# State-space outputs woven into the second attention, with one operand laid out in DRAM beforehand

## The chip, the cores and the metric

The kernel runs on one core of a Trainium2 chip. The metric is the device time of one execution in microseconds (us); the time of a kernel is the median of several executions. TensorE (PE) multiplies matrices into PSUM, ScalarE (ACT) applies functions and copies, VectorE (DVE) does elementwise work and reductions, GpSimd (POOL) does some elementwise work and issues DMAs, and SyncE (SP) issues most DMAs. Each engine runs its own instructions strictly in order and waits on semaphores of the others.

## The reference, cut to what matters

Two blocks follow one another on 512 rows of 1024 columns. The first has two layers (windowed attention, gated linear attention), each with an MLP. The second block mixes an attention and a state-space model through gates, then runs a mixture of experts. The part that the change touches is the middle of the second block:

```python
h = rms_norm_2(x, mix_norm_gain[i])
proj = h @ w_in[i]
...
gate = jax.nn.sigmoid(proj[..., 3 * D_ATTN + D_SSM:] + b_gate[i])
gate = gate.reshape(bsz, l, N_BRANCH, D_MODEL)
y_attn = chunked_relpos_attention(q, k, v, q_gain[i], k_gain[i], rel_bias[i])
y_ssm = s5_ssm_glu(u, ssm_lambda_re[i], ssm_lambda_im[i], ...)
wb = w_branch[i]
merged = (gate[:, :, 0] * (y_attn @ wb[:D_ATTN])
          + gate[:, :, 1] * (y_ssm @ wb[D_ATTN:]))
x = x + merged @ w_out[i]
```

`chunked_relpos_attention` has 8 heads: scores plus a bias, softmax, values. `s5_ssm_glu` runs a linear recurrence over time, reads its outputs out of the states and the inputs, and applies `z = gelu(y)`, then `z * sigmoid(z @ w_glu + b_glu)`.

## The kernel before

All products run as three matmuls of a split pair (`hi` and `lo`), so every 1 MB weight unit is loaded by SP (L214), cast by ACT (`whi`, L221) and subtracted by DVE (`wlo`, L222) before TensorE uses it (L240 to L252). Two `raw`, two `whi` and two `wlo` buffers are in turn. A scheduler with a timeline of its own fixes, when the kernel is built, the order of instructions on each engine; the program's order and Python generators give it the candidates, and on the chip each engine then follows its list in order.

**Constants.** `SSM.constants` is a generator that the second MLP steps through as filler. It leaves in DRAM the tables `w1`, `g` and `k`; `k` has the shape [16, 32, 15, 16] and holds the response of the state-space model to inputs within 8 time steps, with zeros for the future (L1344, and eight stores at L1347).

**Attention of the second block.** `block2_mix` first makes q, k, v and the recurrence's inputs, then runs eight heads. `scores(h)` loads the bias tile `tb` (SP, L1538), splits q and k (ACT L1542, L1545; DVE L1543, L1547), and in four steps multiplies (PE L1555, L1556), adds the bias and takes the maximum (DVE L1558), and takes the exponential (ACT L1563). `values` takes two heads: it scales the probabilities (DVE L1573), transposes them (PE L1581), copies them out of PSUM (ACT and DVE, L1582) and multiplies with V (PE L1585). Between these steps `gate_unit` computes the 16 gate tiles, 24 matmuls each on `hl`, and POOL stores them to DRAM (L1532). The loop asks for one gate tile in every second step of a head, so two for each head:

```python
for n, _ in enumerate(scores(h)):
    if n % 2:
        next(last, None)
    else:
        next(gen, None)
```

**Branches.** After the attention, `fetch` loads gate tiles back (SP, L1629; four buffers), and `branch` multiplies the attention's output `ya` with a branch weight, 12 matmuls for each of 8 rows of `mT`; ACT applies the sigmoid (L1637) and DVE the product (L1660). `ssm.load` brings `G` (two DMAs of 1 MB, L1405) and `W3` (eight DMAs of 256 KB, L1408, whose runs in DRAM are 512 bytes long) into SBUF. After rows 6 and 7 of `mT`, `ssm.outputs` computes the state-space outputs in two halves (Q = 0 and 1): TensorE multiplies the states with `G` (L1423) and the inputs with `W3` (L1427) into two banks, ACT and DVE copy them to `Y` (L1431), TensorE turns `Y` (L1435), and ACT applies gelu into `zT` (L1437). `parts` splits `zT` into the pair `z` (L1648, L1649). Then follow the products `z @ w_glu` with their sigmoid (48 matmuls), which give `ys`, the products of `ys` with the other branch weights (96 matmuls), the output projection and the mixture of experts.

Of the kernel before, what the change touches and what calls it, by code (L numbers as in the profile page):

```python
# [19 lines left out]
P = 128  # L20
# [1165 lines left out]
class SSM:  # L1186


    def __init__(self, K):
        self.K = K  # L1190
        self.w1 = K.dram.tile([P, 2, 16, P], F32, name="ssm_w1")
        self.g = K.dram.tile([P, 2, 16, P], F32, name="ssm_g")
        self.k = K.dram.tile([16, 32, 15, 16], F32, name="ssm_k")
        self.a8 = K.c.tile([P, 2, 2, 16], F32, name="ssm_a8")

    def constants(self, tp):
# [149 lines left out]
        for q in range(8):  # L1346
            nc.gpsimd.dma_start(self.k.rearrange("c (a q) l x -> q c a (l x)", q=8)[q][:, :, 7 * 16:],  # L1347
                                kk[16 * q:16 * q + 16])

    def inputs(self, zp, sp, u_rows):  # L1350

# [46 lines left out]

    def load(self, sp, between):

        nc = self.K.nc
        self.G = sp.tile([P, 2, 16, P], F32, name="ssm_g2", bufs=1)
        self.W3 = sp.tile([P, 32, P], F32, name="ssm_w3", bufs=1)
        for part in range(2):
            nc.sync.dma_start(self.G[:, part], self.g[:, part])  # L1405
        between()
        for t in range(8):
            nc.sync.dma_start(self.W3[16 * t:16 * t + 16].rearrange("p g (t c) -> p g t c", t=8),  # L1408
                              self.k[:, :, 7 - t:15 - t, :])

    def outputs(self, sp, Q, zT):

        K, Z, UT, G, W3 = self.K, self.Z, self.UT, self.G, self.W3
        nc, a, mm = K.nc, K.nc.scalar, K.nc.tensor.matmul
        b = [K.bank() for _ in range(2)]
        for ii in range(4):
            os = [(8 * Q + 4 * h + ii, [b[g][64 * h:64 * h + 64, ii * P:ii * P + P] for g in range(2)])
                  for h in range(2)]
            for part in range(2):
                for g in range(2):  # L1420
                    s = slice(64 * g, 64 * g + 64)
                    for i, o in os:
                        mm(o[g], Z[s, 0:64, part, i], G[s, part, i],  # L1423
                           start=part == 0, stop=False, skip_group_check=True)
            for g in range(2):
                for i, o in os:
                    mm(o[g], UT[:, 2 * i + g, :], W3[:, 2 * i + g, :],  # L1427
                       start=False, stop=True, skip_group_check=True)
        Y = sp.tile([P, 8, P], F32, tag="ssm_y", name=K.nm("Y"), bufs=1)
        for g, e in enumerate((a.copy, K.nc.vector.tensor_copy)):  # L1430
            e(Y.rearrange("p t (i g c) -> p g t i c", g=2, c=16)[:, g],  # L1431
              b[g].rearrange("p (i t c) -> p t i c", i=4, t=8))
        b = K.bank2()
        for t in range(8):
            nc.tensor.transpose(b[:, t * P:t * P + P], Y[:, t, :], K.ident)  # L1435
        for h in range(2):
            a.activation(zT[:, 2 * Q + h].rearrange("p (j t) -> p t j", t=8),  # L1437
                         b.rearrange("p (t h j) -> p h t j", t=8, h=2)[:, h], AF.Gelu_apprx_tanh)


def block2_mix(K, X, hl, ssm, out):
# [6 lines left out]
    with ExitStack() as left:  # L1448
# [85 lines left out]

        with K.right("at2", 2) as ap:
            def scores(h):
# [57 lines left out]

            def gates(c0, c1):
                for c in range(c0, c1):
                    yield from gate_unit(c)

            last, done, gen = iter(()), [], gates(0, 8)
            for h in range(8):  # L1600
                for n, _ in enumerate(scores(h)):
                    if n % 2:
                        next(last, None)
                    else:
                        next(gen, None)
                if h % 2:
                    for _ in last:
                        pass
                    last = values(*done[-2:])
# [5 lines left out]
        z_close.close()  # L1615

        K.h_close.close()
        K.sides = {"left": "left", "right": "right"}
# [23 lines left out]
        zs.push(sz_close)  # L1642
        gl = zs.enter_context(K.left("ssmz", 2))
        z = K.pair(gl, "z", [P, 4, L])

        def parts(Q):
            d = slice(2 * Q, 2 * Q + 2)
            return (nc.scalar.copy(z[0][:, d], zT[:, d]).ins,  # L1648
                    v.tensor_sub(z[1][:, d], zT[:, d], z[0][:, d].bitcast(F32)).ins)  # L1649

        with K.left("ssmr", 2) as sp:
            for r in range(4):
                fetch(r)
            ssm.load(sp, lambda: [fetch(r) for r in range(4, 8)])
            for c in range(2):
                w = K.unit(A["w_br"][c])
                for m in range(4):
                    f = 4 * c + m
                    b, g = branch(w, ya, m, f, f)
                    v.tensor_mul(mT[:, f, :], b, g)  # L1660
                    if c and m in (2, 3):
                        ssm.outputs(sp, m - 2, zT)
                        turned = parts(m - 2)
        yo = left.enter_context(K.left("b2o"))
# [449 lines left out]
```

## Time and profile before

| | us |
|---|---|
| runs of the kernel before | 2270.74, 2275.36, 2281.77 |
| median | 2275.36 |
| the profiled execution | 2268.23 |
| its span on the core | 2266.2 |

| engine | busy us | share of the span |
|---|---|---|
| PE (matmul) | 2138.9 | 94% |
| PEld (weight load) | 1769.3 | 78% |
| DVE | 1390.6 | 61% |
| ACT | 971.2 | 43% |
| POOL | 334.8 | 15% |

The profiled execution is 7.1 us under the median. The span runs from the first instruction to the last, and 2.0 us of the execution lie outside it. The busy share is an average over stages with different limits; what a stage is worth is read from the stretch of time that it covers, which the rows further below do. Times in rows are counted from the start of the span. The attention's gates end near 1861 us, its last value product near 1898 us, and the products on `ys` begin near 1957 us.

### The profile page before, as it was taken

To read this page: it belongs to the slowest core of one execution; us is meant where nothing else is said; L and a number is where in the kernel's file an instruction comes from. 1 tells how busy PE (TensorE), PEld (TensorE's weight loads), DVE (VectorE), ACT (ScalarE), POOL (GpSimd) and SP (SyncE) were. 2 spreads that over 40 slices of the span, in tenths; PEclk is the share of its full clock that TensorE was granted. 3 is DMA by queue.
4 is the path that set the end of the run, shared out by engine and by line. 5 is a ranking of instruction groups with operands and counts; after the bars stand their busy time and mean duration, and the time that the engine had idled before them with its cause. 6 is when DMAs were issued, how large, how long until landed. Compare 5 with 4: busy or idle time off the path is not lost. (4 is left out here: it accounts for less than half of the span.)

```text
span 2266.2 us, 30706 instructions
## 1 busy us (share of the span) xinstructions
PE 2138.9 (94%) x12088; PEld 1769.3 (78%) x12088; DVE 1390.6 (61%) x2436; ACT 971.2 (43%) x1512; POOL 334.8 (15%) x453
## 2 busy tenths in 40 slices
PE   7999999999999999999989999999899997897996
PEld 5876668888888888789977887888799874686875
DVE  4666654999644444631794597555646754547985
ACT  5446656421121222542554632322353453535874
POOL 0035622112000000510000000000220100012332
PEclk9999999999999999999999999999999998998998
DMA  7112231557321121211211224232322435468993
GB/s 291 64 39 98 82 149 38 195 189 255 122 75 56 56 75 56 72 38 59 93 38 38 88 93 149 106 104 84 120 94 94 154 122 115 174 237 278 331 298 105
DMA packets 57970, 279.12 MB, mean 123 GB/s; under 512 B 9248, under 2 KB 13744, under 8 KB 32992
## 3 DMA queue, kind: packets, MB, share of 16 engines
q1 hardware_dynamic: 38048, 219.39, 27.4%
q0 software_dynamic: 18768, 55.04, 7.7%
q10 hardware_dynamic: 1008, 2.70, 0.4%
q8 instruction: 96, 1.57, 0.3%
q14 instruction: 50, 0.41, 0.1%
HBM read 264.54 MB, written 24.08 MB: 127 GB/s over the span
## 5 line engine op out<-in xcount | busy, mean ns | idle before, releaser
L221 ACT CAST whi<-raw 128x2048 fp32r<-128x2048 f32 x106 | 202.4, 1909 | 559.3 <-PE b L252 389.1
L222 DVE TENSOR_TENSOR wlo<-raw,whi 128x2048 fp32r<-128x2048 f32 x106 | 246.0, 2322 | 223.4 <-ACT whi L221 222.1
L250 PE MATMUL b<-hl,whi 128*128 128x512 f32 (+1 forms) x736 | 284.1, 386 | 2.3 <-DVE t L323 1.5
L248 PE MATMUL b<-hl,whi 128*128 128x512 f32 (+1 forms) x736 | 283.0, 385 | 0.8 <-ACT whi L221 0.8
L252 PE MATMUL b<-hl,wlo 128*128 128x512 f32 (+1 forms) x736 | 281.6, 386 | 0.0
L815 DVE TENSOR_TENSOR acc<-acc,b 128x512 f32<-128x512 f32 x280 | 180.8, 682 | 156.0 <-PE b L252 155.7
L248 PE MATMUL b<-whi,hid 128*128 128x512 f32 x640 | 215.5, 395 | 2.5 <-ACT whi L221 1.9
L250 PE MATMUL b<-wlo,hid 128*128 128x512 f32 x640 | 216.8, 394 | 0.0
L252 PE MATMUL b<-whi,hid 128*128 128x512 f32 x640 | 215.1, 395 | 0.0
L250 PEld LDWEIGHTS b<-hl,whi 128*128 128x128 f32 x736 | 139.1, 189 | 30.3 <-issue 2.9
L248 PEld LDWEIGHTS b<-hl,whi 128*128 128x128 f32 x736 | 139.1, 189 | 30.1 <-ACT whi L221 1.3
L252 PEld LDWEIGHTS b<-hl,wlo 128*128 128x128 f32 x736 | 139.3, 189 | 28.3 <-issue 0.2
L1970 DVE TENSOR_TENSOR wlo<-raw,whi 128x2048 fp32r<-128x2048 f32 x57 | 129.8, 2287 | 27.7 <-ACT whi L1970 27.7
L252 PEld LDWEIGHTS b<-whi,hid 128*128 128x128 f32 x640 | 120.3, 188 | 27.9
L248 PEld LDWEIGHTS b<-whi,hid 128*128 128x128 f32 x640 | 119.2, 188 | 29.0 <-ACT whi L221 2.1
L250 PEld LDWEIGHTS b<-wlo,hid 128*128 128x128 f32 x640 | 120.5, 188 | 27.4
L1970 ACT CAST whi<-raw 128x2048 fp32r<-128x2048 f32 x57 | 108.4, 1912 | 10.7 <-PE b L242 10.6
L627 POOL TENSOR_TENSOR p<-p,t 128x512 f32<-128x512 f32 (+2 forms) x96 | 92.5, 972 | 62.8 <-DVE t L626 62.2
L402 DVE CUSTOM_DVE_ANT_0 junk<-mw,cb 128x1024 bf16<-128x1024 f32 x80 | 97.6, 1220 | 3.6 <-DMA mw<-in_w_modT_dram 2.9
L240 PE MATMUL b<-whi,hl 128*128 128x256 f32 x320 | 91.3, 285 | 2.3 <-ACT qr L1478 2.3
L241 PE MATMUL b<-wlo,hl 128*128 128x256 f32 x320 | 91.4, 286 | 0.0
L242 PE MATMUL b<-whi,hl 128*128 128x256 f32 x320 | 91.2, 285 | 0.0
(602 smaller groups left out, 4709.8 us busy)
## 6 DMA issues: line engine op xcount, KB each, us to landing
raw<-in_w_e_dram SPq DMA_DIRECT2D x57, 1024.0 KB, 7.0
raw<-in_w_mlp_in_dram SPq DMA_DIRECT2D x32, 1024.0 KB, 5.1
raw<-in_w_mlp_out_dram SPq DMA_DIRECT2D x32, 1024.0 KB, 4.7
mw<-in_w_modT_dram POOLq DMA_DIRECT2D x56, 512.0 KB, 4.5
raw<-in_w_mod_dram SPq DMA_DIRECT2D x20, 1024.0 KB, 6.3
raw<-in_w_in_dram SPq DMA_DIRECT2D x16, 1024.0 KB, 4.8
raw<-in_gla_in_dram SPq DMA_DIRECT2D x12, 1024.0 KB, 4.8
raw<-in_w_o_dram SPq DMA_DIRECT2D x8, 1024.0 KB, 4.7
```

The lines of the kernel that those rows point to most:

```text
L221: ins = self.nc.scalar.copy(hi, r).ins
L222: ins = ins, (self.nc.gpsimd if pool else self.nc.vector).tensor_sub(lo, r, hi.bitcast(F32)).ins
L240: mm(out, ah, bh, start=start, stop=False)
L241: mm(out, ah, bl, start=False, stop=False)
L242: mm(out, al, bh, start=False, stop=stop)
L248: mm(o, ah, b, start=start, stop=False)
L250: mm(o, ah, b, start=False, stop=False)
L252: mm(o, al, b, start=False, stop=stop)
L402: v.tensor_tensor_reduce(junk, w, cb[b], 1.0, 0.0, ALU.mult, ALU.add, to[:, k, b:b + 1])
L627: nc.gpsimd.tensor_mul(p[:, :n], p[:, :n], den.to_broadcast([P, n]))
L815: nc.vector.tensor_add(a, a, bs[n])
L1970: ins = K.nc.scalar.copy(hi, r).ins, K.nc.vector.tensor_sub(lo, r, hi.bitcast(F32)).ins
```

## The change

**Where the outputs run.** `SSM.outputs` becomes a generator that receives its two banks, and the attention's filler is now first all gates, then `ssm.load`, then both halves of the outputs. The filler is asked in every step of a head, so four times for each head: the 16 gates go with heads 0 to 3, and the 12 steps of the outputs with heads 4 to 7. The banks are those of the gates (`gbank`), and the turned `Y` goes through the same two banks, 4 tiles to a bank, with a gelu for each half bank. `Y` takes a `whi` buffer of the weight stream. `G` and `W3` go into the memory of `hl`, which is given up when the last gate is done; the attention's own buffers (`at2`) move to the other side of SBUF, and so do the buffers of `z`.

**The operand in DRAM.** At the end of `constants`, eight DMAs on POOL's queue copy pieces of `k` within DRAM to `k8`, in the layout of `W3`, so that `W3` is loaded by one DMA of 2 MB with 16 KB runs.

**The branch loop.** All 8 gate rows are fetched ahead, without the loads of `G` and `W3` between them; `parts` is called in the first rows of the branch.

```diff
+        self.k8 = K.dram.tile([P, 32, P], F32, name="ssm_k8")
...
+        for t in range(8):
+            nc.gpsimd.dma_start(self.k8[16 * t:16 * t + 16].rearrange("p g (t c) -> p g t c", t=8),
+                                self.k[:, :, 7 - t:15 - t, :])
...
-        between()
-        for t in range(8):
-            nc.sync.dma_start(self.W3[16 * t:16 * t + 16].rearrange("p g (t c) -> p g t c", t=8),
-                              self.k[:, :, 7 - t:15 - t, :])
+        nc.sync.dma_start(self.W3, self.k8)
...
-        b = K.bank2()
-        for t in range(8):
-            nc.tensor.transpose(b[:, t * P:t * P + P], Y[:, t, :], K.ident)
-        for h in range(2):
-            a.activation(zT[:, 2 * Q + h].rearrange("p (j t) -> p t j", t=8),
-                         b.rearrange("p (t h j) -> p h t j", t=8, h=2)[:, h], AF.Gelu_apprx_tanh)
+        yield
+        for x in range(2):
+            for t in range(4):
+                nc.tensor.transpose(b[x][:, t * P:t * P + P], Y[:, 4 * x + t, :], K.ident)
+            for h in range(2):
+                a.activation(zT[:, 2 * Q + h].rearrange("p (j t) -> p t j", t=8)[:, 4 * x:4 * x + 4],
+                             b[x].rearrange("p (t h j) -> p h t j", t=4, h=2)[:, h], AF.Gelu_apprx_tanh)
+        yield
...
+        def ssm_outputs():
+
+            K.h_close.close()
+            ssm.load(sr.enter_context(tc.tile_pool(name="ssmr", bufs=1, side=K.sides["right"])))
+            for Q in range(2):
+                yield from ssm.outputs(gbank, Q, zT)
+
-        with K.right("at2", 2) as ap:
+        with K.left("at2", 2) as ap:
...
-            def gates(c0, c1):
-                for c in range(c0, c1):
+            def fill():
+                for c in range(8):
                     yield from gate_unit(c)
-
-            last, done, gen = iter(()), [], gates(0, 8)
+                yield from ssm_outputs()
+
+            last, done, gen = iter(()), [], fill()
             for h in range(8):
                 for n, _ in enumerate(scores(h)):
                     if n % 2:
                         next(last, None)
-                    else:
-                        next(gen, None)
+                    next(gen, None)
...
-        with K.left("ssmr", 2) as sp:
-            for r in range(4):
-                fetch(r)
-            ssm.load(sp, lambda: [fetch(r) for r in range(4, 8)])
-            for c in range(2):
-                w = K.unit(A["w_br"][c])
-                for m in range(4):
-                    f = 4 * c + m
-                    b, g = branch(w, ya, m, f, f)
-                    v.tensor_mul(mT[:, f, :], b, g)
-                    if c and m in (2, 3):
-                        ssm.outputs(sp, m - 2, zT)
-                        turned = parts(m - 2)
+        for r in range(8):
+            fetch(r)
+        for c in range(2):
+            w = K.unit(A["w_br"][c])
+            for m in range(4):
+                f = 4 * c + m
+                b, g = branch(w, ya, m, f, f)
+                v.tensor_mul(mT[:, f, :], b, g)
+                if c == 0 and m < 2:
+                    turned = parts(m)
```

The order of the instructions follows from the scheduler, so three places are shown as they stand in the two built kernels. The first is ACT at the gelu of the first half. Before, it stands among the sigmoids of the branch (`g`); one table load serves both halves:

```order
L1637 ACTIVATE g_16816<-g_16816,small 128x512
L1431 COPY Y_16705<-b_16655 128x32x16
L1637 ACTIVATE g_16818<-g_16818,small 128x512
L1437 ACT_TABLE_LOAD
L1437 ACTIVATE zT<-b_2867_16708 128x8x64 x2
L1648 CAST z_16505<-zT 128x1024
L1431 COPY Y_16786<-b_16736 128x32x16
L1437 ACTIVATE zT<-b_2872_16789 128x8x64 x2
```

Now, in the change's line numbers, it stands among the exponentials of the sixth and seventh heads (`p`, L1576) and the copies of transposed probabilities (`pt`, L1595):

```order
L1433 COPY Y_16319<-b_15434 128x32x16
L1605 CAST ya_13682<-b_2636_15433 128x512
L1595 COPY pt_16496<-b_15436 128x384
L1440 ACT_TABLE_LOAD
L1440 ACTIVATE zT<-b_15434 128x4x64 x2
L1576 ACT_TABLE_LOAD
L1576 ACTIVATE p_16420,t_16412<-s_16416,t_16418 128x128
L1440 ACT_TABLE_LOAD
L1440 ACTIVATE zT<-b_15435 128x4x64 x2
L1576 ACT_TABLE_LOAD
L1576 ACTIVATE p_16440,t_16412<-s_16436,t_16438 128x256
L1595 COPY pt_16549<-b_15436 128x256
```

Four table loads stand within these rows, and two more follow at the second half's gelu, some ten instructions on. The second place is TensorE in the change at the same point: the turning of `Y` (L1438), a score product (L1568, L1569), two transposes (L1594), and the first products of the second half into the same two banks:

```order
L1594 MATMUL b_15437<-ident,p_16377 128x128
L1438 MATMUL b_15434<-ident,Y_16319 128x128 x4
L1438 MATMUL b_15435<-ident,Y_16319 128x128 x4
L1568 MATMUL b_2635_15432<-KH_2800_16404,Q_2799_16403 128x256
L1569 MATMUL b_2635_15432<-KL_2801_16405,Q_2799_16403 128x256
L1594 MATMUL b_15436<-ident,p_16252 128x128
L1594 MATMUL b_15436<-ident,p_16272 128x128
L1424 MATMUL b_15434<-ssm_g_16186,ssm_z 64x128 x4
L1428 MATMUL b_15434<-ssm_w_16187,ssm_ut 64x128 x2
```

The bank `b_15434` is written by the turning, read by the first gelu, and written again by the second half, so TensorE's list passes through ACT's list above. The third place is SP's queue after the last bias tiles of the attention. Before:

```order
L1538 DMA tb_16315<-in_rel_dram 128x512
L1629 DMA g_16510<-gates_d 128x512
L1629 DMA g_16512<-gates_d 128x512
L1629 DMA g_16514<-gates_d 128x512
L1629 DMA g_16516<-gates_d 128x512
L1405 DMA ssm_g_16518<-ssm_g 128x2048 x2
L1408 DMA ssm_w_16519<-ssm_k 16x32x128 x3
L1629 DMA g_16522<-gates_d 128x512
```

Now:

```order
L1551 DMA tb_16297<-in_rel_dram 128x512
L1410 DMA ssm_g_16186<-ssm_g 128x2048 x2
L1411 DMA ssm_w_16187<-ssm_k_8449 128x4096
L1551 DMA tb_16400<-in_rel_dram 128x512
L1551 DMA tb_16519<-in_rel_dram 128x512
L214 DMA raw_16822<-in_w_glu_dram 128x2048
L214 DMA raw_16900<-in_w_br_dram 128x2048
L1641 DMA g_16651<-gates_d 128x512
```

`G` and `W3` have moved ahead of the bias tiles of the last two heads (`tb_16400`, `tb_16519`), and nothing stands between the gate rows any more.

## Rows read from the trace of the kernel before

**Rows 1.** Windows: busy us and instructions of each engine by stage, with clock and DMA.
```profile
core 0: us, PE busy (x) PEld busy (x) DVE busy (x) ACT busy (x) POOL busy (x), PEclk, DMA share, GB/s
1760.90:1861.00 100.10, 100.10 (x470) 78.97 (x468) 67.63 (x210) 50.23 (x92) 9.68 (x22) 1.00 0.41 142
1861.00:1885.30 24.30, 19.72 (x87) 11.83 (x86) 17.41 (x56) 15.37 (x37) 0.74 (x2) 0.79 0.18 65
1885.30:1898.00 12.70, 10.58 (x49) 5.19 (x47) 4.78 (x13) 2.06 (x6) 0.00 (x0) 1.00 0.01 2
1898.00:1911.40 13.40, 13.40 (x60) 10.62 (x59) 5.62 (x6) 6.44 (x7) 0.00 (x0) 1.00 0.92 279
1911.40:1941.70 30.30, 19.05 (x214) 13.94 (x213) 5.81 (x7) 12.47 (x15) 0.00 (x0) 0.83 0.88 190
```

**Rows 2.** Timeline of PE from 1911 us on: start, us, instruction, idle before and releaser.
```profile
1917.84 1.12 PE L1423 MATMUL b<-ssm_g,ssm_z 64*64 64x128 f32 x8 [5.74 <-DVE mT L1660]
1929.15 0.66 PE L1427 MATMUL b<-ssm_w,ssm_ut 128*64 128x128 f32 x8 [4.19 <-DMA ssm_w<-ssm_k]
1941.66 0.73 PE L248 MATMUL b<-z,whi 128*128 128x512 f32 x2 [0.37 <-ACT z L1648]
...
1951.00 1.19 PE L248 MATMUL b<-z,whi 128*128 128x512 f32 x4 [1.90 <-ACT z L1648]
...
1957.42 0.73 PE L248 MATMUL b<-ys,whi 128*128 128x512 f32 x2 [0.33 <-ACT ys L1676]
```

**Rows 3.** DMA issues from 1893 to 1962 us: size of each, median us to landing.
```profile
g<-gates_d SPq DMA_DIRECT2D x14, 256.0 KB, 10.0
ssm_g<-ssm_g SPq DMA_DIRECT2D x2, 1024.0 KB, 7.8
ssm_w<-ssm_k SPq DMA_DIRECT2D x8, 256.0 KB, 12.1
```

**Rows 4.** Timeline of PE at the attention's end.
```profile
1860.86 0.40 PE L248 MATMUL b<-ya,whi 128*128 128x512 f32 x1
...
1890.49 1.08 PE L1585 MATMUL b<-pt,v 128*64 128x512 f32 x4 [0.79 <-DVE pt L1582]
1891.50 0.92 PE L1581 MATMUL b<-ident,p 128*128 128x128 f32 x4
```

**Rows 5.** Groups by line, ACT, 1898 to 1960 us: busy us, mean ns, idle before.
```profile
L221 ACT CAST whi<-raw 128x2048 fp32r<-128x2048 f32 x3 | 5.7, 1897 | 0.6 <-PE b L250 0.6
L1437 ACT ACTIVATE zT<-b 128x512 f32<-128x512 f32 x4 | 4.2, 1155 | 6.1 <-PE b L1435 6.1
L1637 ACT ACT_TABLE_LOAD x2 | 2.6, 1283 | 0.0
L1648 ACT CAST z<-zT 128x1024 fp32r<-128x1024 f32 x2 | 2.1, 1044 | 0.1
L1437 ACT ACT_TABLE_LOAD x1 | 1.3, 1283 | 0.0
```

**Rows 6.** Timeline of ACT: the last exponential, and a table load with its neighbours.
```profile
1887.62 0.19 ACT L1563 ACTIVATION_READ_ACCUMULATOR p<-s,t 128x1 f32 x1
...
1950.85 1.90 ACT L221 CAST w_br<-raw 128x2048 fp32r<-128x2048 f32 x1
1952.77 1.28 ACT L1637 ACT_TABLE_LOAD   x1
1954.07 1.34 ACT L1637 ACTIVATE g<-g,small 128x512 f32<-128x512 f32 x2
```

**Rows 7.** The store of zeros into `k` by POOL: issue in ns, landing in us.
```profile
L1344 POOL DMA_DIRECT2D ssm_k<-st x1: 754/754/754, 1260.3 to 1260.3; - x1
...
DMA to landing us min/median/max: 8.1/8.1/8.1
```

**Rows 8.** Second MLP: a weight load's issue (SP), the second cast after it, POOL's next work.
```profile
1523.49 0.33 SPq L214 DMA_DIRECT2D raw<-in_w_mlp_in_dram  x1
...
1541.54 1.91 ACT L221 CAST whi<-raw 128x2048 fp32r<-128x2048 f32 x1 [3.62 <-PE b L250]
...
1612.74 4.62 POOL L222 TENSOR_TENSOR ya<-raw,ya 128x2048 fp32r<-128x2048 f32 x1 [93.13 <-ACT ya L221]
```

More of the change, by code (lines that the diff above doesn't have):

```diff
@@ L1397, in ahead, with load @@
         self.us = [K.unit(W[6 + i], to=[flat(x) for x in t], pool=i == 0) for i, t in enumerate((self.ya, (zT, UT)))]
-    def load(self, sp, between):
+    def load(self, sp):
         nc = self.K.nc
@@ L1405, in load, with outputs @@
             nc.sync.dma_start(self.G[:, part], self.g[:, part])
-        between()
-        for t in range(8):
-            nc.sync.dma_start(self.W3[16 * t:16 * t + 16].rearrange("p g (t c) -> p g t c", t=8),
-                              self.k[:, :, 7 - t:15 - t, :])
-    def outputs(self, sp, Q, zT):
+        nc.sync.dma_start(self.W3, self.k8)
+    def outputs(self, b, Q, zT):
         K, Z, UT, G, W3 = self.K, self.Z, self.UT, self.G, self.W3
         nc, a, mm = K.nc, K.nc.scalar, K.nc.tensor.matmul
-        b = [K.bank() for _ in range(2)]
         for ii in range(4):
@@ L1428, in outputs @@
                        start=False, stop=True, skip_group_check=True)
-        Y = sp.tile([P, 8, P], F32, tag="ssm_y", name=K.nm("Y"), bufs=1)
+            yield
+        Y = K.w.tile([P, 2048], F32, tag="whi", name=K.nm("Y"))[:, :1024].rearrange("p (t c) -> p t c", t=8)
         for g, e in enumerate((a.copy, K.nc.vector.tensor_copy)):
@@ L1432, in outputs @@
               b[g].rearrange("p (i t c) -> p t i c", i=4, t=8))
-        b = K.bank2()
-        for t in range(8):
-            nc.tensor.transpose(b[:, t * P:t * P + P], Y[:, t, :], K.ident)
-        for h in range(2):
-            a.activation(zT[:, 2 * Q + h].rearrange("p (j t) -> p t j", t=8),
-                         b.rearrange("p (t h j) -> p h t j", t=8, h=2)[:, h], AF.Gelu_apprx_tanh)
+        yield
[5 more added lines that the diff above has]
+                             b[x].rearrange("p (t h j) -> p h t j", t=4, h=2)[:, h], AF.Gelu_apprx_tanh)
+        yield
 def block2_mix(K, X, hl, ssm, out):
@@ L1533, in gate_unit @@
                 yield
-        with K.right("at2", 2) as ap:
+        sr = ExitStack()
+        def ssm_outputs():
[4 more added lines that the diff above has]
+        with K.left("at2", 2) as ap:
             def scores(h):
@@ L1615, in block2_mix @@
         z_close.close()
-        K.h_close.close()
+        sr.close()
         K.sides = {"left": "left", "right": "right"}
@@ L1642, in block2_mix @@
         zs.push(sz_close)
-        gl = zs.enter_context(K.left("ssmz", 2))
+        gl = zs.enter_context(K.right("ssmz", 2))
         z = K.pair(gl, "z", [P, 4, L])
```

## The prediction

> **What bounds the kernel now.** I read the busy shares first: TensorE is busy for 94% of the span, so only its idle stretches can be won. Then the windows by stage, which show where they lie. Until the last gate TensorE is busy all the time [rows 1]: in 1760.9 to 1861.0 the gates fill whatever the attention leaves. Behind it come 37.0 us in which three heads are left and few matmuls to put between them: 24.3 us at 19.72 busy and a granted clock of 0.79, then 12.7 at 10.58. The products on `ya` that follow run without a gap (13.4 us). The next 30.3 us hold the state-space outputs with 19.05 busy at a clock of 0.83. The timeline of TensorE says what it waits for there: 5.74 us for a product of the branch, 4.19 for `W3`, and later 1.90 for `z` [rows 2]. The list of transfers shows why `W3` is late: eight transfers of 256 KB take 12.1 us each to land, among 1 MB transfers that take 7.8 [rows 3]. So from the last gate (1860.9, the first `ya` product [rows 4]) to the first product on `ys` (1957.4 [rows 2]) there are 96.5 us. These 96.5 us are what the change rebuilds; ahead of them and behind them the orders of all engines agree but for eight DMAs on POOL.
>
> **The gates' end.** Four gates to a head use up the gates by the fourth head, so less of the attention stands ahead of the last gate. Counted in TensorE's two orders, 4 score pairs, 19 transposes and 3 value products have moved behind it. A transpose takes 0.92 / 4 = 0.23 us; a product of 512 columns 1.08 / 4 = 0.27, and the moved ones are of 128 to 512 columns, so about 0.16 [rows 4]. That is 19 x 0.23 + 11 x 0.16 = 6.1 us, bounds 4 and 8. TensorE is full there, so all of it counts: the gates end at **1854.9**.
>
> **The tail.** Let T be the time from the last gate to the last value product: 37.0 us before. It now holds four heads, three pairs of values, both halves of the outputs and 27 of the 96 products on `ya` (33 before). Two sums bound T.
>
> By TensorE: 19.72 + 10.58 = 30.3 busy before; less 6 `ya` products at 13.4 / 57 = 0.235 us each (57 of them fill the third window), plus 6 for what was moved in, plus the outputs, which are 19.05 less 13 `ya` products (3.1), so 16.0: in all 50.9. This is a floor, rather high, since part of it was measured at the lower clock.
>
> By ACT: its list in the tail is a chain, since the outputs use the two gate banks over and over. The first gelu must free a bank before TensorE may write the second half into it, and behind the second gelu on ACT stand the last exponentials of head 6 and all of head 7. I take it in three pieces.
> (a) From the last gate to the first copy of `Y`: two heads at 24.3 / 3 = 8.1 us, 16.2, and some 3 of the first half's 8 us of products that find no gap. About 19.
> (b) From there to the last exponential. Two copies to `Y`: no row has them; four gelus on 512 columns take 1155 ns each [rows 5], a copy of that size in the nearest rows about half, so 1.1 for two. Gelu in eight half pieces: 4 x 1.155 = 4.6. Table loads: ACT's new list has six in this stretch, at 1283 ns [rows 5]: 7.7. Two casts at 1897 ns: 3.8. The exponentials and copies of about two heads: ACT was busy 15.37 + 2.06 = 17.4 over three heads [rows 1], less a cast and half a microsecond for other things, 5.0 a head, so 10. The sum is 27.2, and with 1.5 for waits between TensorE and ACT, 29.
> (c) From the last exponential (1887.8, [rows 6]) to the last value product (1898.0, the end of the second window) 10.2 us, as before.
> T is 19 + 29 + 10.2 = 58, and with a microsecond for the two DVE copies that stand ahead of head 6's last reductions, **59**. TensorE would be busy for 50.9 / 59 = 86% of it (82% before), so both sums can hold. The unknown in it is how much of ACT's list waits: with TensorE full and a little over, 54; with waits of 0.3 us at each of some 25 turns more, 66.
>
> **The table loads.** Before the change the branch and the outputs needed three, now the stage needs seven. In the trace the load at 1952.77 takes 1.28 us and starts 0.02 us after the cast ahead of it; the sigmoid starts 0.02 us after its end [rows 6]. So each of the six is put down at 1.28, nothing around it.
> The Trainium skill ("ScalarE: Activation LUTs", What ACT_TABLE_LOAD costs) gives about 1.28 us for the load, as here, and a drain of about 1.38 us beside it. By that figure the six would add an estimated 8.3 us to the chain.
>
> **Behind the tail.** 96 - 27 = 69 `ya` products at 0.235 are 16.2 us, then 48 on `z` at the same rate 11.2; 1 us for the first gate row, 0.7 for the wait before `ys` (0.33 before). `z` is long ready, so its two waits fall away. In all 29.1: `ys` begins at 1854.9 + 59 + 29.1 = **1943.0** instead of 1957.4, a gain of 14.4 us. T pays for itself up to 73.
>
> **The transfers.** `G` and `W3` may start only when the last gate has read `hl`, and the bias tiles of heads 6 and 7 queue behind them on SP. 4 MB at 279 GB/s [rows 1] are 15 us, so they have landed by about 1870; the first `G` product is wanted some 8 us after the last gate (2 MB are there in 7.5), `W3` and the bias tile some 16. It just fits: nothing, upper bound 7 us. The gate rows behind wait for nothing but their order.
>
> **The copies on POOL** stand behind the stores of `k` at about 1519 us. POOL issues the store of zeros in 754 ns and has landed it after 8.1 us [rows 7]; eight such issues are 6 us, and POOL's next work is at 1612.74, after an idle stretch of 93 us [rows 8]. What they could delay is the weight stream of the second MLP: a load issued at 1523.49 belongs to a cast at 1541.54, some 18 us ahead. Eight copies of 256 KB in two directions, at 12 us each if they ran like `W3`'s pieces, lie in that stretch; a load would have to take over 18 us before TensorE saw it. Put at nothing; bounds 0 and 4.
>
> **The sum.** The profiled execution took 2268.23: 2268.2 - 14.4 = 2253.8. It lies 7.1 under the median of the runs, so on the median's footing **2261**. For T of 54 to 66 the forecast's own range is 2256 to 2268.
>
> **Rivals.**
> *TensorE stays full.* The waits on ACT hide wholly under three heads' matmuls. Then T is the floor, 51, or a few us less at the full clock: gain 22 or more, 2253 to 2249. For it: there are 60 us of work and only two heads' dependences. Against: in the two windows before, with 33 filler products, TensorE still idled for 6.7 of 37 us.
> *Late operands.* 4 MB and the bias tiles arrive later than reckoned, since the window with 279 GB/s was the best of the stage; 7 us more: 2268.
> *The drain.* The page's rule on grouping functions by table set speaks against this change, which splits one gelu run into separate ones among exponentials. As a mechanism of this kernel: ACT would stand still about as long again around each of six loads, 8 us more, 2269. No gap of that kind stands beside the load in [rows 6], so it gets little. This is the same section of the Trainium skill, "ScalarE: Activation LUTs".
> *Slower: ACT's order blocks the tail.* Its work in the tail is 4 x 5.0 + 1.1 + 7.7 + 4.6 + 3.8 = 37 us. In the old tail ACT was busy for 17.4 of 37.0 us, 47%, because each exponential waits for a score and each copy for a transpose, in strict order. If the turns with TensorE keep that share, T is 79, `ys` begins 6 us later than before: 2282. It decides where T passes 73. Against it: the loads, casts and gelus wait for little.
> *The copies are not free*, or the change moves less than the orders say: TensorE waits for weights in the second MLP for 5 to 15 us and the gain is gone: 2266 to 2276.
>
> **Chances.** Forecast 0.57, TensorE full 0.16, late operands 0.09, drain 0.05, blocked tail 0.09, copies 0.04. About 0.5% (11.4 us) is what a measurement of this kernel can tell from no change, so faster means under 2264. Of the forecast about two thirds lie there (0.39), with all of the full TensorE (0.16) and a little of the others: 0.56. Slower has most of the blocked tail: 0.08. The rest, 0.36, is within the bound. The range of 2247 to 2275 takes in all but the blocked tail and the outer ends.
>
> **What would show it.** Right: last gate near 1855; six table loads between it and the last exponential, ACT busy for over 60% of that stretch; last value product near 1914; no wait of TensorE over 1 us from there to `ys` at about 1943; the second MLP unmoved. The steps would be wrong if TensorE's waits in the tail were for `ssm_g`, `ssm_w` or `tb` (late operands), if gaps of about a microsecond stood beside the loads on ACT (drain), or if waits on `b`, `zT` and `p` from ACT made up over 25 us (blocked tail). The forecast as a whole fails if `ys` begins later than 1950 or before 1936.

## The result, and the profile after

The changed kernel took 2254.86 us (median of 11 runs, 2246.94 to 2265.91), the kernel before 2273.46 (11 runs, 2270.53 to 2281.77). The ratio is 0.9919, interval 0.9901 to 0.9936: faster by 0.8%. The prediction was 2261 in a range of 2247 to 2275. The profiled execution of the changed kernel took 2246.94, its span is 2245.1 (before 2268.23 and 2266.2); these two lie 7.9 and 5.2 us under the medians.

The windows of the change by stage: up to the last gate, to the first copy of `Y`, to the last exponential, to the last value product, to the first product on `ys`.

```profile
core 0: us, PE busy (x) PEld busy (x) DVE busy (x) ACT busy (x) POOL busy (x), PEclk, DMA share, GB/s
1760.90:1854.70 93.80, 93.80 (x435) 75.54 (x432) 58.17 (x188) 41.65 (x74) 9.05 (x21) 1.00 0.39 138
1854.70:1873.60 18.90, 16.80 (x156) 10.88 (x157) 12.88 (x44) 11.48 (x29) 0.83 (x3) 0.91 0.70 264
1873.60:1904.20 30.60, 23.98 (x192) 16.41 (x188) 16.87 (x45) 26.57 (x44) 0.00 (x0) 1.00 0.20 70
1904.20:1914.30 10.10, 7.93 (x36) 3.75 (x37) 3.42 (x9) 0.64 (x2) 0.00 (x0) 1.00 0.00 0
1914.30:1942.10 27.80, 27.54 (x119) 22.06 (x118) 18.27 (x19) 21.87 (x27) 0.00 (x0) 1.00 0.70 246
```

They answer to [rows 1]. The last gate ends 6.2 us earlier, the tail grows from 37.0 to 59.6 us, and behind it 27.8 us run almost without a gap, where before 13.4, 30.3 and 15.7 followed. From the last gate to `ys` it is 87.4 us instead of 96.5: with the 6.2 a gain of **15.3 us**. The whole stretch before, the whole stretch now, and the tail alone now:

```profile
1861.00:1957.40 96.40, 75.65 (x458) 51.06 (x456) 40.21 (x88) 46.13 (x75) 0.74 (x2) 0.89 0.48 123
1854.70:1942.10 87.40, 76.25 (x497) 53.09 (x497) 51.44 (x115) 60.55 (x102) 0.83 (x3) 0.98 0.44 160
1854.70:1914.30 59.60, 48.71 (x380) 31.03 (x380) 33.16 (x96) 38.69 (x75) 0.83 (x3) 0.97 0.32 120
```

TensorE is about as busy in both (75.65 us before, 76.25 now), and idle time fell from 20.8 to 11.2. The busy time now holds 39 more matmuls, those that moved behind the last gate, at a granted clock of 0.98 instead of 0.89: so a part of the gain, about as large as the 6.2 us that they took ahead of the gate, shows as a higher clock.

The list of TensorE's waits of the change from 1855 to 1914 us (us in total, times, longest) shows what is left of the idle time:

```profile
PE b L248 <- ACT zT L1440: 2.8, 1, 2.8
PE b L1568 <- DVE t L1571: 2.0, 1, 2.0
PE b L1598 <- DVE pt L1595: 1.4, 3, 0.8
PE b L1424 <- DMA ssm_g<-ssm_g: 1.2, 1, 1.2
PE b L1424 <- ACT zT L1440: 1.1, 2, 0.9
PE b L1594 <- DVE p L1586: 0.9, 1, 0.9
PE b L1428 <- DMA ssm_w<-ssm_k: 0.5, 1, 0.5
PE b L1568 <- DVE Q L1556: 0.3, 1, 0.3
PE b L1438 <- ACT pt L1595: 0.2, 1, 0.2
```

The waits of [rows 2] for `mT`, `ssm_w` and `z` (5.74, 4.19, 1.90) are gone. Of the other **5.8 us** of the spans' 21.1, 5.6 lie where nothing was expected, behind the last instruction of all, a store that POOL issues. First the kernel before (span 2266.2), then the change (2245.1), from POOL's timeline:

```profile
2251.41 1.55 POOL L2014 DMA_INDIRECT out_dram<-xy,tab  x1 [4.05 <-DMA out_dram<-x,tab]
```
```profile
2235.99 1.55 POOL L2023 DMA_INDIRECT out_dram<-xy,tab  x1 [3.74 <-DMA out_dram<-x,tab]
```

From its end to the end of the span it was 13.2 us, and is now 7.6. The trace's records say where it went: two instructions of POOL itself that end the program, `INC_SWDGE_SEM`, 1.69 us before and 0.55 now, and the longest `DRAIN` of the last line (durations in ns, shortest, median and longest), before and now:

```profile
L2110 POOLq DRAIN  x3: 46/109/6195, 2259.1 to 2265.9; - x3
L2119 POOLq DRAIN  x3: 46/109/1544, 2242.8 to 2244.9; - x3
```

Between the start of `ys` and the end of that store the work is the same, and it took 295.5 us before and 295.4 now. That this is equal is luck: over all 14 profiles of this document it is from 291.3 to 305.8, so single profiles settle a stage, and not the whole time.

### The profile page after: what moved, and what is told of

It is laid out like the page before. It is cut to its first block, busy times and chain, and to the rows that moved or that the text cites. A ratio compares the mean times of both kernels' runs of the same rounds, so it can differ in the third digit from the quotient of the medians.

```text
span 2245.1 us, 30692 instructions
## 1 busy us (share of the span) xinstructions
PE 2130.6 (95%) x12088; PEld 1766.9 (79%) x12088; DVE 1390.4 (62%) x2436; ACT 975.7 (43%) x1520; POOL 336.1 (15%) x461
## 5 line engine op out<-in xcount | busy, mean ns | idle before, releaser
L252 PEld LDWEIGHTS b<-whi,hid 128*128 128x128 f32 x640 | 120.3, 188 | 27.8
L248 PEld LDWEIGHTS b<-whi,hid 128*128 128x128 f32 x640 | 119.2, 188 | 29.1 <-ACT whi L221 2.1
L1979 ACT CAST whi<-raw 128x2048 fp32r<-128x2048 f32 x57 | 108.2, 1910 | 10.2 <-PE b L242 10.2
L240 PE MATMUL b<-whi,hl 128*128 128x256 f32 x320 | 90.6, 283 | 2.3 <-ACT qr L1482 2.3
L623 DVE CUSTOM_DVE_ANT_0 p<-b,mask,nsink 128x512 f32<-128x512 f32 (+2 forms) x96 | 67.5, 704 | 40.0 <-PE b L619 25.7
```

What stands on the lines that cost most here:

```text
L240: mm(out, ah, bh, start=start, stop=False)
L248: mm(o, ah, b, start=start, stop=False)
L252: mm(o, al, b, start=False, stop=stop)
L623: nc.vector.tensor_tensor_reduce(p[:, :n], S[:, a0:a0 + n], added[:, z:z + n], -1.0, ns, ALU.add, ALU.min, nmx)
L1979: ins = K.nc.scalar.copy(hi, r).ins, K.nc.vector.tensor_sub(lo, r, hi.bitcast(F32)).ins
```

## The experiments

The theory at first was the prediction's: the middle of the tail is a chain on ACT, so its table loads cost what they take. "The change" below is the changed kernel; stretches are from one profile each, times are medians against runs of the kernel before on the same chip.

**1. No table loads (e1).** gelu is the identity in the tail; this one function is left out of the computation.

```diff
-                             b[x].rearrange("p (t h j) -> p h t j", t=4, h=2)[:, h], AF.Gelu_apprx_tanh)
+                             b[x].rearrange("p (t h j) -> p h t j", t=4, h=2)[:, h], AF.Identity)
```

> The changed kernel with the eight gelu pieces of the tail replaced by the identity function, which needs no table load, so that the six loads of the tail are gone while the order on every engine stays (the computation is changed in this one function). In the changed kernel the stretch from the first copy of Y to the last exponential took 30.6 us with ACT busy 26.57 and TensorE 23.98. Theory (ACT's list is the chain there): the stretch shrinks by 5 to 7 us, to where TensorE's own 24 us stop it; the products on ys begin near 1936 instead of 1942.1, and the kernel is 5 to 7 us faster than the changed one. Rival (TensorE's work sets the tail, ACT's waits are slack): under 2 us. Rival (each load costs a pause beside its 1.28 us): 10 us or more, with the stretch shorter than 24 us impossible only because of TensorE, so waits there vanish entirely.

2248.49 us, ratio 0.9884 (0.9857 to 0.9911); 6 us under the change by the medians, as the theory has it, but with intervals that overlap, and the values that reach the mixture of experts are others here. What can be told from the tail, where the matmuls are the same, is in the traces. The windows of its trace from the first copy of `Y` to the last exponential, and of its whole tail:

```profile
1874.30:1903.40 29.10, 24.90 (x192) 17.36 (x188) 16.24 (x42) 18.07 (x38) 0.00 (x0) 0.94 0.21 73
1855.60:1913.70 58.10, 48.81 (x380) 31.26 (x380) 33.27 (x96) 30.12 (x69) 0.83 (x3) 0.97 0.33 123
```

ACT lost 8.5 us of work (38.69 to 30.12 over the tail), the tail 1.5. All of that is in the stretch from the first copy of `Y` to the last exponential, 29.1 for 30.6, with TensorE busy 0.9 us longer in it at a lower clock (0.94 against 1.00); so even without that it is 2.4, and the theory's 5 to 7 is not there. TensorE waited on `zT`, which ACT's gelus write, only for 3.9 us in the list above, and 1.8 of it is still there. TensorE's 48.8 us over the tail are the same. Why the medians differ by more than the tail isn't shown.

**2. The gelus after the last exponential (e2).** In the tail `Y` is only copied; two gelus follow on `zT`.

```diff
-            for h in range(2):
-                a.activation(zT[:, 2 * Q + h]...[:, 4 * x:4 * x + 4], b[x]...[:, h], AF.Gelu_apprx_tanh)
+            for h, e in enumerate((a.copy, K.nc.vector.tensor_copy)):
+                e(zT[:, 2 * Q + h]...[:, 4 * x:4 * x + 4], b[x]...[:, h])
...
+            for Q in range(2):
+                d = slice(2 * Q, 2 * Q + 2)
+                tc.add_manual_dep(nc.scalar.activation(zT[:, d], zT[:, d], AF.Gelu_apprx_tanh).ins, lastexp[0].name,
...
```

> A candidate for a better version: in the tail the turned Y is only copied to zT (half by ACT, half by DVE), and two gelus of 1024 columns run after the last exponential, where ACT was busy 0.64 us of 10.1. Of the seven loads of the stage two are left. Theory: the stretch from the first copy of Y to the last exponential loses the six loads (7.7 us) and 2 of 4.3 us of gelu on ACT, and shrinks to about 24 to 26 us; the gelus (about 4.2 us and a load of 1.3) fit in the last 10 us but for 1 to 2 us; the kernel is 4 to 6 us faster than the changed one. Rival (TensorE sets the tail): within 2 us. Rival (the gelus delay the last copies of probabilities by their whole 5.5 us): no gain.

2250.27 us, ratio 0.9898 (0.9877 to 0.9919). The tail is 57.0 us, from the last gate to `ys` 84.8 (87.4). TensorE no longer waits for `zT`, but 4.0 us at one stroke for the eighth head's `Q`, which DVE makes behind a `wlo` of 2.29 us; the granted clock of the tail is 0.94 (0.97). A wait has changed its name. Of the gain that was expected, 4 to 6 us, the medians show 4.6, within the noise of the two, and the traces 2.6.

**3. W3 in pieces (e3).** The change with `W3` loaded by the eight old DMAs and no `k8`.

```diff
-        nc.sync.dma_start(self.W3, self.k8)
+        for t in range(8):
+            nc.sync.dma_start(self.W3[16 * t:16 * t + 16].rearrange("p g (t c) -> p g t c", t=8),
+                              self.k[:, :, 7 - t:15 - t, :])
```

> The changed kernel without the copy in DRAM: W3 is loaded by eight DMAs of 256 KB with runs of 512 bytes, in its new place. Theory: W3 arrives some 10 us later than 1869.4 us (before the change it was needed at 1925 and came at 1929, behind 2 MB of G); TensorE waits for ssm_w for 4 to 8 us in the tail, and the kernel is 4 to 8 us slower than the changed one, still faster than the one before. Rival (the layout in DRAM is worth nothing in the new place, because TensorE has scores and values to do meanwhile): within 2 us.

2271.97 us, ratio 1.0002 (0.9984 to 1.0020): the whole gain is gone. The first product with `W3` on TensorE, then from the view of the tile its issues on SP (ns, first and last start) and the median landing:

```profile
1880.79 1.12 PE L1425 MATMUL b<-ssm_w,ssm_ut 128*64 128x128 f32 x8 [10.06 <-DMA tb<-in_rel_dram]
...
L1407 SPq DMA_DIRECT2D ssm_w<-ssm_k x8: 677/1955/3162, 1855.4 to 1868.3; - x8
...
DMA to landing us min/median/max: 10.8/12.9/13.9
```

SP needs 14.9 us to issue the eight, and the bias tiles queue behind. The profile names such a tile, `tb`, as the releaser; the last piece of `W3`, issued from 1868.3 us on, lands at about the same time. The tail grows by 14.4 us to 74.0, 11.0 of it idle time of TensorE and 3.4 its busy time, at a clock of 0.86 instead of 0.97. 5.5 more are lost behind the last store (13.1 us from it to the end of the span, as before the change).

**4. The copy alone (e4, and e12 for a second profile).** The kernel before with `k8` and one DMA for `W3`.

> The kernel before with the copy in DRAM alone: the order of the tail and of the branch is the old one, W3 is one DMA of 2 MB. Theory: the wait of 4.19 us for W3 in the outputs goes, and with it some us of low clock; 3 to 6 us faster than before, and the second MLP is unmoved although the eight copies run in it. Rival (the copies cost the second MLP something): TensorE is idle for more than 1 us between 1500 and 1600 us, and the gain is under 2 us.

2264.82 us, ratio 0.9961 (0.9943 to 0.9978). TensorE's wait for `ssm_w` falls to 1.8 us and the 5.74 us for `mT` are gone, but `ys` begins 94.9 us after the last gate, 1.5 earlier than before. The outputs' matmuls ran at a lower clock (1910.6 to 1937.2: 0.74, against 0.83 in [rows 1]) and so took what the waits gave: over the 94.9 us TensorE is idle for 11.9 us instead of 20.8, and busy for 83.0 at 0.82 instead of 75.7 at 0.89.

> The kernel before with the copy in DRAM alone, a second profile. In its first profile the products on ys began 94.9 us after the last gate (96.4 before), only 1.5 us earlier, while the medians lay 0.4% apart, some 9 us; TensorE was busy for 83.0 us of the 94.9 at a granted clock of 0.82, against 75.7 at 0.89 before. If the clock of this stretch differs from one execution to the next, the stretch is 88 to 92 us here with a clock nearer 0.89, and the medians are explained; if it repeats at 94 to 96, this edit gives under 2 us there and the rest of the difference of the medians lies elsewhere, or in the spread of the runs.

2260.76 us, ratio 0.9947 (0.9929 to 0.9966), and again 96.4 us from the last gate to `ys` (1863.6 to 1960.0), with 0.74 from 1911 to 1937. So in the old order the single load gives 0 to 1.5 us in its own stage. Both profiles end 7.3 to 7.5 us after the last store: 5.7 to 5.9 us are won there. That makes 6 to 7 of the 8 to 13 us between the medians; the rest is not traced, and the unchanged stretch behind `ys` took 299.9 us in the one profile and 291.3 in the other. So this edit alone gives 8 to 13 of the 18.6 us of the change by the medians, most of what is traced of it at the program's end.

**5. The change again (e5).**

> The changed kernel as it is, once more on the chip of the others, for a second profile. What belongs to the change must come back within a microsecond: last gate at 1854.8, first copy of Y at 1873.6, last exponential at 1904.1, last value product at 1914.4, products on ys from 1942.1. What lies behind (303.0 us from there to the end of the span, against 308.8 before) is expected to differ by some us from one execution to the next, since the two profiles of before and after differ in it though no order changed there.

2254.59 us, ratio 0.9926 (0.9898 to 0.9953). The last gate ends at 1852.2, so the work ahead of it moves by 2.6 us between executions, and the times counted from the start did not come back within a microsecond. The stretches did: the tail is 59.5 us and `ys` begins 87.3 after the last gate, as in the first profile. From the first score product of this attention to the last gate it is 87.1 us in both (93.9 before), so the pace moved the gates' end by 6.8 us, and from that product to `ys` it is 174.5 in both instead of 190.3, a gain of 15.8. From `ys` to the end of the span it is 312.2 us here, against 303.0 in the first profile, though both run the same kernel. Behind the last store it is 7.4 us.

**6. The old pace with the outputs at the attention's end (e6).**

```diff
                     if n % 2:
                         next(last, None)
-                    next(gen, None)
+                    else:
+                        next(gen, None)
```

> The changed kernel with the old pace, one gate tile in every second step of a head: the gates reach to the eighth head again, and the outputs run in and behind the last pair of values, with W3 in one piece and the branch's products around them. Theory (the weaving fills the tail's idle TensorE, and needs the heads): gates end at 1861, the outputs' turns (copy, turn, gelu, second half) stand bare behind the attention; products on ys begin 4 to 8 us later than with the change, near 1948. Rival (only the early loads and the single W3 count): within 2 us of the change.

2252.30 us, ratio 0.9906 (0.9877 to 0.9936): within noise of the change. The gates end at 1862.2, `ys` begins 82.6 us later, at 1944.8. So neither theory nor rival holds as put: `ys` is 2.7 us later in the trace than with the change, not 4 to 8, and the whole time does not show it. Two gates or four to a head hardly matter once the outputs stand ahead of the branch. The rival isn't excluded by it: no run has the early loads and the single `W3` without any weaving.

**7. The new pace alone (e7).** The kernel before with four gate tiles to a head.

```diff
                     if n % 2:
                         next(last, None)
-                    else:
-                        next(gen, None)
+                    next(gen, None)
```

> The kernel before with the new pace alone: four gate tiles to a head, outputs in the branch, W3 in eight pieces. Theory (an empty tail costs what the gates gain): the gates end near 1855, but four heads stand bare behind them, 45 us instead of 37 to the last value product, so that ends near 1900 and the kernel is 2 to 4 us slower than before. Rival (the earlier end of the gates is itself the gain): 5 us faster than before.

2282.00 us, ratio 1.0039 (1.0024 to 1.0055). The gates end at 1855.1; the last value product comes 50.1 us later (37.1 before), `ys` at 1966.0. An empty tail costs 13 us and the pace gives 6: slower, by more than expected.

**8. POOL instead of DVE for two `wlo` (e8).** On top of e2, `K.unit(A["w_br"][c], pool=True)`.

> The version with the gelus behind the last exponential, and with the wlo of the first two branch weights subtracted by POOL instead of DVE. With the table loads gone the tail shrank from 59.6 only to 57.0 us, and TensorE's longest wait in it became one of 4.0 us for Q of the eighth head, which DVE made behind a wlo of 2.29 us. Theory now (TensorE's 48.8 us in strict order, and whatever engine is late for it: ACT with the loads, DVE without them): the wait for Q falls by about 2.3 us and the second wlo (2.28) no longer stands ahead of the eighth head's scores; the tail is 52 to 55 us, and the kernel 2 to 4 us faster than the version with DVE. Rival (POOL's subtraction, 4.6 us as in the second MLP, is late for the first products with wlo): TensorE waits there instead and nothing is gained.

2254.76 us, ratio 0.9925 (0.9899 to 0.9950), no faster than the change; the tail is 63.2 us. The theory missed; nothing is gained, as the rival said, but not by its wait. TensorE's wait for `Q` grew to 10.1 us. DVE's two preparations, and POOL's subtractions beside them:

```profile
1887.91 4.56 DVE L1562 TENSOR_TENSOR KL<-kT,KH 64x512 fp32r<-64x512 f32 x2 [0.26 <-ACT KH L1560]
1892.50 4.87 DVE L1558 TENSOR_TENSOR Q<-qT,Q 64x512 fp32r<-64x512 f32 x1
```
```profile
1886.69 4.53 POOL L222 TENSOR_TENSOR wlo<-raw,whi 128x2048 fp32r<-128x2048 f32 x1 [13.67 <-ACT whi L221]
1892.28 4.55 POOL L222 TENSOR_TENSOR wlo<-raw,whi 128x2048 fp32r<-128x2048 f32 x1 [1.05 <-ACT whi L221]
```

In e2 the same DVE instructions took 1.39 (two) and 0.69 us. Here each ends 0.5 to 1.3 us behind a subtraction of POOL (1891.2 and 1896.8), so DVE stood still until POOL was done. The Trainium skill ("SBUF — State Buffer", Who interferes with whom) has the rule: a DVE instruction with two inputs in SBUF and a GpSimd instruction that reads SBUF exclude each other for the whole instruction. The two rows agree.

**9. The weight splits behind the eighth head (e9 on e2, e10 on the change).**

```diff
-            w = K.unit(A["w_br"][c])
+            w = K.unit(A["w_br"][c], after=(lastm if c else lastq))
```

`lastq` holds the last head's two splits of Q, and `lastm` its last maximum; on each engine the weight's split is put behind them.

> The version with the gelus behind the last exponential, and with two weight splits moved in order: the first branch weight's whi and wlo come behind the eighth head's Q on ACT and DVE, the second's wlo behind the eighth head's last maximum. POOL has no part in it, so DVE keeps its usual durations. Theory (TensorE's 48.8 us in strict order plus whichever engine is late): the wait of 4.0 us for Q falls under 2, the eighth head's reductions no longer stand behind a wlo of 2.28; the tail falls from 57.0 to between 52 and 55 us, products on ys begin 84.8 - 2 to 5 us after the last gate, the kernel 2 to 5 us faster than with the gelus moved alone. Rival (another wait takes its place: the first products on ya now wait for wlo): within 1 us.

> The changed kernel with the two weight splits moved in order, the gelus where the change put them. Theory: the waits of 2.0 us for the eighth head's reductions go, the wait of 2.8 for zT stays or falls by the 1.9 us of the cast that stood ahead of it; the tail falls from 59.6 to 56 to 58 us. Rival (ACT's loads are the chain): 59 or more.

e9: 2251.22 us, ratio 0.9910 (0.9889 to 0.9931), a tail of 60.9 us; e10: 2253.89, ratio 0.9911 (0.9895 to 0.9928), a tail of 63.8. Both theories missed. In e9 the wait for `Q` did fall, to 1.6 us, but another took its place, as the rival said, though not at `wlo`: the second `wlo` now stood ahead of the last scaling (TensorE waits 2.3 us for `p`, and 2.0, as in the change, for the last head's reductions). In e10 the tail lies in its rival's range, 59 or more, but not because of ACT, which ends 2.9 us of TensorE's waits there (4.1 in the change). In e10 TensorE's waits are not longer than the change's, and its busy time is, 53.27 us against 48.71 for the same 380 matmuls. Windows of e10, then of the change at the same place, show where:

```profile
1889.20:1893.20 4.00, 1.45 (x8) 0.90 (x7) 3.94 (x5) 3.97 (x6) 0.00 (x0) 1.00 0.01 2
1893.20:1897.20 4.00, 3.76 (x10) 2.89 (x10) 0.02 (x1) 3.97 (x6) 0.00 (x0) 0.57 0.73 262
1905.20:1909.20 4.00, 3.15 (x11) 1.14 (x11) 1.25 (x3) 0.37 (x1) 0.00 (x0) 0.76 0.81 262
1909.20:1913.20 4.00, 3.56 (x11) 1.65 (x11) 0.98 (x2) 0.27 (x1) 0.00 (x0) 0.50 0.00 0
```
```profile
1890.70:1894.70 4.00, 1.25 (x5) 1.05 (x6) 3.35 (x5) 3.94 (x7) 0.00 (x0) 1.00 0.48 158
1894.70:1898.70 4.00, 2.37 (x13) 1.79 (x11) 2.36 (x2) 3.97 (x5) 0.00 (x0) 1.00 0.27 111
```

After a stretch in which TensorE was busy for 1.45 of 4 us, the granted clock of e10 fell to 0.57 and later to 0.50, which is the lower level of 1.2 GHz; the change, after one of 1.25, stayed at full speed.

**10. The old pace and the late gelus (e11).** e6 and e2 together; the gelus follow when the outputs are through.

> The old pace (one gate tile in every second step) with the outputs at the end of the attention and the gelus on zT at once, so that two loads of the stage are left. With the old pace the products on ys began 82.6 us after the last gate, of which TensorE waited 2.0 for a gelu and 1.9 for G. Theory (TensorE's work counts, the pace hardly): 80 to 82 us, the kernel within 2 us of the version with the gelus moved and four gates to a head. Rival (a second half that waits for copies on ACT behind a gelu of 1024 columns): 83 or more.

**2246.44 us, ratio 0.9876 (0.9859 to 0.9893): the fastest**, some 8 us under the change. From the last gate (1863.2) to `ys` it is 76.5 us, less than expected. TensorE's waits, and one window of e6, then of e11:

```profile
PE b L1424 <- DMA ssm_g<-ssm_g: 1.7, 2, 1.1
PE b L252 <- DVE wlo L222: 1.0, 1, 1.0
PE b L1600 <- DVE t L1576: 0.9, 1, 0.9
PE b L1424 <- DVE zT L1440: 0.7, 1, 0.7
```
```profile
1890.00:1894.00 4.00, 2.79 (x38) 2.20 (x38) 0.00 (x0) 3.96 (x7) 0.00 (x0) 0.92 0.00 0
1894.00:1906.00 12.00, 12.00 (x74) 6.22 (x69) 2.84 (x7) 2.66 (x5) 0.00 (x0) 0.50 0.01 2
```
```profile
1890.00:1894.00 4.00, 3.26 (x41) 2.25 (x41) 2.81 (x9) 3.77 (x6) 0.00 (x0) 1.00 0.00 0
1894.00:1906.00 12.00, 11.05 (x91) 6.48 (x90) 4.67 (x6) 5.11 (x7) 0.00 (x0) 1.00 0.01 2
```

In e6 TensorE waited 2.0 us for a gelu, from 1889.2 to 1891.2 us, and the 12 us from 1894 on ran at half clock: 74 matmuls. In e11 that wait is gone, and 91 ran. From the last gate to `ys`, e6 and then e11:

```profile
1862.20:1944.80 82.60, 77.02 (x458) 52.55 (x457) 44.09 (x91) 49.35 (x83) 0.68 (x2) 0.88 0.46 166
1863.20:1939.70 76.50, 71.73 (x457) 50.51 (x457) 46.71 (x96) 47.08 (x80) 0.68 (x2) 0.96 0.49 179
```

5.3 of the 6.1 us between the two are TensorE's busy time for the same matmuls, at a clock of 0.96 instead of 0.88.

## Why the prediction was right, and where its reason was not

**The time** is right: 6 us under the forecast, inside the range, on the forecast's side. By the medians the gain is 18.6 us for the 14.4 foretold.

**The gates' end**: 1854.9 foretold, 1854.7 measured. That it is so near is luck, since the second profile has 1852.2; counted from the first score product the move is 6.8 us for the 6.1 foretold, inside its bounds. **Behind the tail**: 29.1 foretold, 27.8 measured; the microsecond for the first gate row and the 0.7 for `ys` were not needed. **The products on `ys`**: 1943.0 and 1942.1.

**The tail** has the foretold length, 59 against 59.6, and in each piece: 19 and 18.9, 29 and 30.6, 10.2 and 10.1. Its reason failed. The step is (b), the sum of ACT's list as a chain. The six loads and ACT's busy 26.57 of 30.6 us are there as it said, and its sign, ACT busy for over 60% up to the last exponential, came true (77%); but e1 took 8.5 us off ACT and the tail lost 1.5. So the right length is luck as far as ACT's sum goes. What the runs show in its place: TensorE's own work of 48.7 us, and some 10 us of waits in its strict order, of which ACT ends 4, DVE 4.6 and transfers 1.7; take one away and another engine is late (e2, e9), and the work itself takes longer where the granted clock is lower (e10, e6). TensorE's sum, the floor of 50.9, was 2 us too high, as the text feared. It has a slip besides: 28 `ya` products stood in the old tail, and not 33, so one and not six was to be taken off and the floor would have been 52.1, 3.4 over the measured work, which ran at a granted clock of 0.97 instead of the 0.79 and 0.83 of [rows 1]. That two sums agreed with T was no proof of either; TensorE's work with some idle time on top, which the prediction gave only as a floor and a share, was the sounder one.

**The table loads** cost 1.28 us and nothing beside it. ACT's timeline of the change around two of them:

```profile
1875.10 1.28 ACT L1440 ACT_TABLE_LOAD   x1
1876.39 1.09 ACT L1440 ACTIVATE zT<-b 128x256 f32<-128x256 f32 x2
1877.49 1.28 ACT L1576 ACT_TABLE_LOAD   x1
1878.79 0.40 ACT L1576 ACTIVATE p<-s,t 128x128 f32<-128x128 f32 x1
```

The gaps are 0.01 to 0.02 us. The pause of about 1.38 us that the Trainium skill names ("ScalarE: Activation LUTs", What ACT_TABLE_LOAD costs) is not there, and that rival falls.

**The transfers** were put at nothing and cost 1.7 us of waits. This held only with the new layout: in pieces `W3` costs 14 us here (e3), twice the 7 of the rival of late operands.

**The copies on POOL** cost nothing, as put: TensorE is busy for 100.00 us from 1500 to 1600 in both kernels, and the eight issues follow the stores of `k` without hurt:

```profile
1524.95 1.89 POOL L1352 DMA_DIRECT2D ssm_k<-ssm_k  x3 [1.94 <-DMA ssm_k<-ssm_kk]
1527.94 3.09 POOL L1352 DMA_DIRECT2D ssm_k<-ssm_k  x5 [1.10 <-issue]
1616.13 4.62 POOL L222 TENSOR_TENSOR ya<-raw,ya 128x2048 fp32r<-128x2048 f32 x1 [85.09 <-ACT ya L221]
```

**Missing** from the sum is the end of the program, 5.6 us; without it the stages gave 15.3 for the 14.4 foretold. **The blocked tail** (T of 79) did not come: its share of 47% for ACT was 65% (38.69 of 59.6).

## What to carry to other kernels

A chain read from one engine's list is shown to bind only when the other engine waits for it: before costing ACT's 29 us, sum the waits that ACT ends on the engine that sets the end. Here that was 4 us, and taking the loads off gave 1.5 of the tail. Work woven into a tail pays by the idle time that it fills, so bring its operands early and in long runs, and let no engine that it turns to be late; the pace of the filler mattered less here. And a wait of 2 us on TensorE went with 6 in all where the clock fell behind it (e6 against e11).

## What the runs showed of the hardware

**The end of the program.** From the end of the last store's instruction to the end of the span it is 13.2, 13.1 and 13.4 us in three profiles (before, e3, e7), and 4.9 to 7.8 us in the other eleven. The step between the two groups lies in two instructions of POOL: `INC_SWDGE_SEM` takes 1.69 us and the `DRAIN` behind it 6.20 in each of the three, 0.55 and 1.54 in each of the eleven, 5.8 us in all. The three are the kernels that load `W3` in eight DMAs of 512-byte runs on SP's queue, but they are also the ones without the eight copies into `k8` on POOL's queue (153 DMAs on it instead of 161). No run has one without the other, so which of the two sets it stays open; that the time is POOL's own speaks for its queue, and the eight loads on SP had been issued over 300 us before the end.

**DVE stands still beside POOL** when both read SBUF in this way (e8): 0.69 us became 4.87.

**The clock** fell to half behind some stretches of little work on TensorE and not behind others as empty (e10 and the change above). What decides between them stays open.
